# Inverting the diagonal blocks of a delta rule: one stream transpose for four blocks, TensorE in source order up to the recurrence, gates moved into the first chunks

## The chip, the cores and the metric

The kernel runs on one core of one Trainium2 chip. The time is device microseconds of one execution of the whole program; what is compared is the median of several executions. The engines are TensorE (PE in the profile: matmuls, and PEld for its weight loads), VectorE (DVE), ScalarE (ACT), GpSimd (POOL) and SyncE (SP, which issues the transfers).

## The reference

Two layers of a decoder trunk for 512 tokens of width 1024 in float32. What matters here is the mixer of each layer:

```python
n = rmsnorm(h)
p = n @ W_in              # RWKV-7 groups, MLA latents (q, kv, rope key), two groups of gates
# RWKV-7, 8 heads of 64: a state with a delta rule
state = state * w_t + (state @ a_t) b_t^T + v_t k_t^T      # a_t = -kk, b_t = kk * iclr
y_t   = state @ r_t
# MLA: 8 heads of causal softmax attention from low-rank latents
h = h + (sigmoid(g_A) * (y_A @ W_oA) + sigmoid(g_B) * (y_B @ W_oB)) @ W_out
h = h + conv_ffn(rmsnorm(h))
```

The 16 gate tiles (128 columns each of g_A and g_B) need only `n` and are read again at the end of the mixer. The attention needs the latents and no result of the delta rule.

## The kernel before, in words

Activations lie transposed, features on partitions and the 512 tokens along the free dimension. A weight unit holds eight blocks of 128 x 128; each projection of 128 columns takes one unit. To keep float32 accuracy each block and each input is split into a high and a low part, and `mm3` runs three matmuls of 512 columns per block, so a unit is 24 matmuls. `unit` and `produce` fetch a unit with SyncE into `raw` (two buffers), ScalarE casts the high part `whi` (line 201), VectorE subtracts to get `wlo` (line 202); at most two units are ready ahead. `wtile` runs a whole unit into an accumulator; `Part` does the same in pieces of n blocks (k-steps) and calls `end` on the last.

A planner orders the instructions of each engine: it simulates the engines with its own costs and, where several instructions could go, takes the one that stands first in the source. Inside `tc.manual_schedule(engines={PE.engine})` TensorE's instructions keep the order of the source; instructions from outside may still be placed among them, and the other engines remain the planner's. The kernel before uses this in three places, none of them in the stage of this change.

The delta rule is computed in 8 chunks of 64 tokens. For each chunk `c` and head, `AM` holds masked score blocks (last written at line 602), `AR` and `BT` the scaled operands, `Z` the values, `St` the states. The stage of the change stands between the four `pair` generators and the attention:

- four latent units `lat0` to `lat3` (line 658 evicts each with the norm's `rstd`), their squares, `tok_sums` on TensorE, `rsqrt_tok` (VectorE line 304, GpSimd line 305, ScalarE line 297) and `spread` (TensorE line 312), which give the two latent norms; the rope products `kp`;
- for each pair of chunks a product of the A_ak blocks with the values (line 676), copied back to `Z` by ScalarE (line 680);
- the inverse of every unit lower triangular 64 x 64 block of `AM`. The four 32 x 32 diagonal blocks (two chunk parities, two halves) are brought into `X` by stream transposes (line 698), 30 steps of forward substitution on VectorE invert them all at once (lines 702 and 704), and further transposes write them back to `AM` and into `T11` (lines 707 and 709). The lower left block is then the join: a first product with `T11` (line 718), copied to `Q` (line 721), a second product (line 725), copied into `AM` (line 729);
- the recurrence over the chunks: the state's product (line 742), its sum with `Z` (745), the inverse (751), a copy to `Z` (753), the state's update (759, 766 or 768);
- four gate units `GATES[4]`, whose eviction is line 462 and whose tanh is line 470, written to memory by SyncE.

Behind it, the attention heads (`heads`, lines 863 to 906), the chunks' outputs and their group norms. The operands of the attention (`qops`, `kvop`) are written into buffers of tag `xa`, which hold the first half of the normalized input that the gates read. `sc` has two PSUM banks, `xyt` one tile of two banks, and there are two accumulators.

Of the kernel before, what the change touches and what calls it, by code (L numbers as in the profile page):

```python
# [9 lines left out]
F32 = mybir.dt.float32  # L10
F32R = mybir.dt.float32r
I32 = mybir.dt.int32
AF = mybir.ActivationFunctionType
# [145 lines left out]
def build(ctx, tc, x, pos, wst, vecd, constd, out):  # L159
# [265 lines left out]
    def mixer(l, ops, nrm, wks):  # L425
        with ExitStack() as mx:
# [220 lines left out]
            with pool(name=f"ti{l}", bufs=2) as ti:  # L647
# [6 lines left out]
                lat = []  # L654
                for i in range(4):
                    ps = wtile(ops)
# [3 lines left out]
                sq = [ti.tile([128, 512], F32, name="lsq", bufs=3) for _ in range(3)]  # L660
                for i in range(3):
                    A.activation(sq[i], lat[i], AF.Square)
                G.tensor_tensor(sq[0], sq[0], sq[1], ALU.add)
                ws = []
                for i, (t, n) in enumerate(((sq[0], 256.0), (sq[2], 128.0))):
                    ssq = sc()
                    tok_sums(ssq, t)
                    ws.append(rsqrt_tok(ssq, n, NORM_EPS, pool=ti, tag=f"nw{i}"))


                for i in range(4):
# [10 lines left out]
                rq = tl.tile([128, 512], F32, name="rq", bufs=1)  # L682
                spread(ws[0], tabs[1], rq, sc)
                rk = ti.tile([128, 512], F32, name="rk", bufs=1)
                spread(ws[1], None, rk, sc)
                V.scalar_tensor_tensor(lat[2], lat[2], vc(l, "kv_norm"), rk, ALU.mult, ALU.mult)
                kp = tl.tile([128, 512], F32, name="kp", bufs=1)
                k2 = ti.tile([128, 512], F32, name="k2", bufs=1)
# [5 lines left out]
                X = ti.tile([128, 32, 32], F32, name="X", bufs=1)  # L694
                T11 = ti.tile([128, 32, 32], F32, name="T11", bufs=1)
                quad = [((0 if e else 64) + 32 * hf, (128 if e else 64) + 32 * hf, hf) for e in range(2) for hf in range(2)]
                for r0, c0, hf in quad:
                    V.transpose(X[r0:r0 + 32], AMu[r0:r0 + 32, :, c0:c0 + 32].rearrange("p u t -> p t u"))  # L698
                for s in range(1, 31):
                    tm = ti.tile([128, 256], F32, name="tm", tag="tm", bufs=2)  # L700
                    tm = tm[:, 0:(31 - s) * s].rearrange("p (a b) -> p a b", b=s)
                    V.tensor_tensor(tm, X[:, s + 1:32, s:s + 1].to_broadcast([128, 31 - s, s]),  # L702
                                    X[:, s:s + 1, 0:s].to_broadcast([128, 31 - s, s]), ALU.mult)
                    V.tensor_tensor(X[:, s + 1:32, 0:s], X[:, s + 1:32, 0:s], tm, ALU.add)  # L704
                V.memset(X.rearrange("p a b -> p (a b)")[:, 0:1024:33], 1.0)
# [5 lines left out]
                half = [(64, 64), (0, 128)]  # L711
                for b in range(2):
                    us = range(16 * b, 16 * b + 16)
                    Q = ti.tile([128, 512], F32, name="Q", bufs=2).rearrange("p (u s) -> p u s", s=32)
                    ps = xyt()[:, b, :]
                    for u in us:
                        for r0, c0 in half:
                            PE.matmul(ps[r0 + 32:r0 + 64, 32 * (u % 16):32 * (u % 16) + 32], AMu[r0:r0 + 32, u, c0 + 32:c0 + 64],
                                      T11[r0:r0 + 32, u, :], start=True, stop=True, tile_position=(r0, r0 + 32))
                    for r0, c0 in half:  # L720
                        (A.copy if r0 else V.tensor_copy)(Q[r0 + 32:r0 + 64], ps[r0 + 32:r0 + 64, :].rearrange("p (u s) -> p u s", s=32))
                    ps = xyt()[:, b, :]
                    for u in us:
                        for r0, c0 in half:
                            PE.matmul(ps[r0:r0 + 32, 32 * (u % 16):32 * (u % 16) + 32], Q[r0 + 32:r0 + 64, u % 16, :],
                                      AMu[r0 + 32:r0 + 64, u, c0 + 32:c0 + 64], start=True, stop=True,
                                      tile_position=(r0 + 32, r0))
                    for r0, c0 in half:
# [41 lines left out]
                for i in GATES[4][1:]:  # L770
                    gate(i, ti)
# [291 lines left out]
```

## Time and profile before

| | |
|---|---|
| Time, median of 3 runs | 1614.26 us (1613.88 to 1615.4) |
| The profiled execution's own time | 1612.19 us |
| Its span, first to last instruction | 1610.4 us |
| TensorE busy | 1571.3 us (98%) |
| VectorE busy | 939.5 us (58%) |
| ScalarE busy | 652.5 us (41%) |
| GpSimd busy | 188.3 us (12%) |
| Mean granted TensorE clock | 0.991 |

Busy time is an average over stages with different limits. The stage of the change lies at 184 to 302 us of the span in layer 0 and at 979 to 1097 us in layer 1. TensorE's matmuls are pipelined, so the duration of one is longer than the distance to the next; the clock column is the share of 2.4 GHz that TensorE was granted, and its levels are 1.2 and 2.4 GHz.

### The profile page before, as it was taken

Reading aid. Unit: us, or ns where it says so; the run is one execution under the profiler, and the core shown is the slowest. Engines: PE = TensorE matmul, PEld = TensorE weight load, DVE = VectorE, ACT = ScalarE, POOL = GpSimd, SP = SyncE. Lnnn points to the kernel's source line nnn. Section 1 sums busy time; section 2 is a strip of 40 time slices with the busy share of each in tenths; the row PEclk is TensorE's granted clock in tenths of the full one; section 3 lists DMA queues with packets and bytes.
Section 4 is the critical chain, followed back from the end, with each engine's and each line's share of the span. In section 5 each row is a group of like instructions: output and inputs, shape, how many; then the busy total and the mean of one; then the engine's idle time right before and its main releaser. Section 6 shows DMA issues by size and latency. Waiting matters only on the chain.

```text
span 1610.4 us, 22362 instructions
## 1 busy us (share of the span) xinstructions
PE 1571.3 (98%) x9036; PEld 1260.7 (78%) x9036; DVE 939.5 (58%) x1474; ACT 652.5 (41%) x988; POOL 188.3 (12%) x158
## 2 busy tenths in 40 slices
PE   8999989999999999999999999899999999999998
PEld 6888766668888888888878887666688888888887
DVE  6578796666555555533346768856665555554333
ACT  6445334573443333422245442346534443333322
POOL 1011101300211101100001110023003110110000
PEclk9999999999999999999999999899999999999999
DMA  6333312225322323233343333212343223223232
GB/s 210 111 105 125 112 60 86 67 66 156 132 92 94 102 92 102 95 106 123 111 139 110 99 98 112 73 47 80 92 145 127 94 92 99 98 92 105 92 99 85
DMA packets 57271, 166.07 MB, mean 103 GB/s; under 512 B 6352, under 2 KB 8528, under 8 KB 57168
## 3 DMA queue, kind: packets, MB, share of 16 engines
q1 hardware_dynamic: 57024, 164.48, 31.0%
q8 instruction: 71, 1.16, 0.3%
q14 instruction: 32, 0.26, 0.1%
q10 hardware_dynamic: 144, 0.16, 0.0%
HBM read 147.32 MB, written 17.30 MB: 102 GB/s over the span
## 4 chain that ended last, share of the span: by engine, by line
PE 89%; DVE 7%; POOL 2%; ACT 1%; issue 1%; DMA 0%; POOLq 0%; DVEq 0%; SPq 0%; ACTq 0%
PE acc L246 26%; PE acc L248 25%; PE acc L247 25%; PE sc L885 2%; PE po L903 2%; PE xy L751 1%; PE pt L896 1%; DVE wlo L202 1%; DVE AM L707 1%; DVE X L698 1%; POOL mu L814 1%; PE m L599 1%; DVE tm L702 1%; DVE X L704 1%; POOL Z L819 1%
## 5 line engine op out<-in xcount | busy, mean ns | idle before, releaser
L246 PE MATMUL acc<-hi,whi 128*128 128x512 f32 (+1 forms) x1910 | 752.5, 394 | 9.1 <-ACT hi L282 5.2
L248 PE MATMUL acc<-hi,wlo 128*128 128x512 f32 (+1 forms) x1910 | 746.6, 391 | 1.1 <-DVE wlo L202 1.1
L247 PE MATMUL acc<-lo,whi 128*128 128x512 f32 (+1 forms) x1910 | 745.2, 390 | 0.0
L201 ACT CAST whi<-raw 128x1024 fp32r<-128x1024 f32 (+2 forms) x249 | 253.5, 1020 | 536.9 <-PE acc L247 472.4
L246 PEld LDWEIGHTS acc<-hi,whi 128*128 128x128 f32 x1910 | 361.0, 189 | 85.3 <-ACT hi L282 5.2
L248 PEld LDWEIGHTS acc<-hi,wlo 128*128 128x128 f32 x1910 | 360.9, 189 | 78.4 <-DVE wlo L202 2.4
L247 PEld LDWEIGHTS acc<-lo,whi 128*128 128x128 f32 x1910 | 361.4, 189 | 73.6 <-issue 1.2
L202 DVE TENSOR_TENSOR wlo<-raw,whi 128x1024 fp32r<-128x1024 f32 (+2 forms) x249 | 308.3, 1240 | 175.0 <-ACT whi L201 174.4
L983 POOL TENSOR_TENSOR c<-c,rstd 128x512 f32<-128x512 f32 x44 | 57.9, 1317 | 403.6 <-ACT c L982 403.6
L976 DVE TENSOR_TENSOR u<-acc,rstd 128x512 f32<-128x512 f32 x44 | 30.4, 692 | 104.7 <-PE acc L248 104.5
L985 DVE TENSOR_TENSOR c<-c,acc 128x512 f32<-128x512 f32 x44 | 30.3, 688 | 86.4 <-POOL c L983 86.4
L982 ACT ACTIVATE c<-c 128x512 f32<-128x512 f32 x44 | 27.8, 632 | 81.7 <-DVE c L981 81.7
L341 POOL TENSOR_TENSOR nacc<-nacc,nsq 128x512 f32<-128x512 f32 x14 | 25.1, 1790 | 201.5 <-ACT nsq L340 201.5
L450 DVE TENSOR_TENSOR cur<-acc,rstd 128x512 f32<-128x512 f32 x28 | 19.1, 690 | 46.9 <-PE acc L248 39.3
L305 POOL TENSOR_TENSOR nv<-nv,cst 128x4 f32<-128x4 f32 (+1 forms) x10 | 10.1, 1011 | 309.1 <-DVE nv L304 309.1
L891 ACT ACTIVATE P<-P,mn 128x128 f32<-128x128 f32 (+3 forms) x64 | 35.6, 556 | 26.2 <-DVE mn L888 22.8
L885 PE MATMUL sc<-K,q 128*128 128x128 f32 (+3 forms) x128 | 44.5, 447 | 0.0
L462 DVE TENSOR_TENSOR gg<-acc,rstd 128x512 f32<-128x512 f32 x28 | 19.2, 685 | 35.8 <-PE acc L248 35.6
L893 ACT ACTIVATE P<-P,mn 128x128 f32<-128x128 f32 (+3 forms) x64 | 34.8, 558 | 8.8 <-DVE mn L892 8.8
L903 PE MATMUL po<-PT,Vt 128*64 128x128 f32 x320 | 37.5, 286 | 0.7 <-DVE PT L898 0.7
L979 ACT ACTIVATE c<-u,vec 128x512 f32<-128x512 f32 x44 | 35.7, 810 | 2.8 <-DVE u L975 2.8
L888 DVE CUSTOM_DVE_ANT_0 P<-sc,cst 128x128 f32<-128x128 f32 (+3 forms) x64 | 30.6, 481 | 9.1 <-PE sc L885 5.2
(240 smaller groups left out, 1396.2 us busy)
## 6 DMA issues: line engine op xcount, KB each, us to landing
raw<-in_w SPq DMA_DIRECT2D x238, 512.0 KB, 3.3
gate_d<-gg SPq DMA_DIRECT2D x32, 256.0 KB, 2.0
AM<-gate_d SPq DMA_DIRECT2D x16, 256.0 KB, 4.8
gb<-gate_d SPq DMA_DIRECT2D x16, 256.0 KB, 3.5
h<-in_x SPq DMA_DIRECT2D x8, 256.0 KB, 4.2
rgate_d<-gt SPq DMA_DIRECT2D x8, 256.0 KB, 2.6
bl_d<-rk SPq DMA_DIRECT2D x8, 256.0 KB, 2.0
bl<-bl_d SPq DMA_DIRECT2D x8, 256.0 KB, 2.7
```

The lines of the kernel that those rows point to most:

```text
L201: A.copy(hi, r)
L202: V.tensor_tensor(lo, r, hi.bitcast(F32), ALU.subtract)
L246: PE.matmul(ps, w[0], xx[0], start=first, stop=False)
L247: PE.matmul(ps, w[0], xx[1], start=False, stop=False)
L248: PE.matmul(ps, w[1], xx[0], start=False, stop=last)
L885: PE.matmul(sp[:, 0:n], qs[hh][:, 128 * b:128 * b + 128], ks[hh][:, 0:n], start=True, stop=True)
L888: V.tensor_tensor_reduce(out=P[:, 0:n], in0=sp[:, 0:n], in1=cst[:, C_CAUS + 512 - n:C_CAUS + 512], scale=-ATT_SCALE, scalar=1e30, op0=ALU. ...
L891: A.activation(P[:, 0:n], P[:, 0:n], AF.Exp, bias=mn[:, 0:1], scale=-1.0, accum_out=mn[:, 1:2])
L893: A.activation(P[:, 0:n], P[:, 0:n], AF.Copy, scale=mn[:, 2:3])
L903: PE.matmul(po[64 * hh:64 * hh + 64, 128 * b:128 * b + 128], Vt[:, kb, 64 * hd:64 * hd + 64], PTs[hh][:, 128 * kb:128 * kb + 128], start=k ...
L979: A.activation(cc, u[:, 2:514], AF.Identity, bias=vc(l, "conv_b", i), scale=vc(l, "conv_w", 2 * FT + i))
L983: G.tensor_tensor(cc, cc, rstd, ALU.mult)
```

## The change

- **One transpose for four blocks.** The four diagonal blocks are first copied side by side into a tile `DX` of 128 partitions, two copies on VectorE and two on ScalarE. One stream transpose of all 128 partitions brings them into `X`, one gives `T11` and one gives `T22`, the inverse in its original orientation. `back` copies `T22` into `AM` on ScalarE, two copies for each chunk parity. The second joining product reads `T22` instead of `AM`. The substitution now stands first in the stage's source.
- **TensorE in source order.** The whole stage, up to and with the recurrence, stands in a `manual_schedule` region for TensorE: three latent units, an A_ak product, sums, the fourth latent in two halves, sums, spread, A_ak, spread, half a gate, A_ak, half a gate, A_ak, a gate, the join with parts of a gate between, the recurrence. The sum of the first two squares is taken by TensorE's accumulation instead of GpSimd.
- **Joining copies.** Both copies of `Q` for each half are on VectorE; of the copies into `AM` one half is ScalarE's and the other VectorE's. Both products for the two halves run one behind the other in `sc` banks.
- **Gates in the first chunks.** The last half of one gate and a whole one are issued two k-steps at a time by `filler`, once behind each of the recurrence's product groups, until they are used up in the third chunk.

```diff
-            with pool(name=f"ti{l}", bufs=2) as ti:
+            with pool(name=f"ti{l}", bufs=2) as ti, tc.manual_schedule(engines={PE.engine}):
+                DX = ti.tile([128, 32, 32], F32, name="DX", tag="dx", bufs=1)
...
+                for r0, c0, hf in quad:
+                    (A.copy if hf else V.tensor_copy)(DX[r0:r0 + 32], AMu[r0:r0 + 32, :, c0:c0 + 32])
+                V.transpose(X, DX.rearrange("p u t -> p t u"))
+                for s in range(1, 31):
...
+                V.memset(X.rearrange("p a b -> p (a b)")[:, 0:1024:33], 1.0)
+                V.transpose(T11.rearrange("p u s -> p s u"), X.rearrange("p t s -> p s t"))
+                T22 = ti.tile([128, 32, 32], F32, name="T22", tag="dx", bufs=1)
+                V.transpose(T22.rearrange("p u t -> p t u"), X)
+                def back(e):
+                    for r0, c0, hf in quad:
+                        if (r0 < 64) == bool(e):
+                            A.copy(AMu[r0:r0 + 32, :, c0:c0 + 32], T22[r0:r0 + 32])
+                back(0)
...
-                G.tensor_tensor(sq[0], sq[0], sq[1], ALU.add)
...
+                def lsum(i, t, n):
+                    ssq = sc()
+                    tok_sums(ssq, t)
+                    return rsqrt_tok(ssq, n, NORM_EPS, pool=ti, tag="lsq", bufs=3)
...
+                parts4 = [Part(ops, lat_end) for _ in range(4)] + [gpart(i) for i in GATES[4]]
+                for i in range(3):
+                    parts4[i].go()
+                a_ak_v(0)
+                w0 = lsum(0, sq[0:2], 256.0)
+                parts4[3].go(4)
+                w1 = lsum(1, sq[2], 128.0)
+                parts4[3].go()
...
+                spread(w0, tabs[1], rq, sc)
+                a_ak_v(1)
...
+                spread(w1, None, rk, sc)
...
+                parts4[4].go(4)
+                a_ak_v(2)
+                parts4[4].go()
+                a_ak_v(3)
+                parts4[5].go()
...
-                for r0, c0, hf in quad:
-                    V.transpose(X[r0:r0 + 32], AMu[r0:r0 + 32, :, c0:c0 + 32].rearrange("p u t -> p t u"))
...
-                for r0, c0, hf in quad:
-                    V.transpose(AMu[r0:r0 + 32, :, c0:c0 + 32].rearrange("p u t -> p t u"), X[r0:r0 + 32])
-                    if hf == 0:
-                        V.transpose(T11[r0:r0 + 32].rearrange("p u s -> p s u"), X[r0:r0 + 32].rearrange("p t s -> p s t"))
-                gate(GATES[4][0], ti)
...
                     for r0, c0 in half:
-                        (A.copy if r0 else V.tensor_copy)(Q[r0 + 32:r0 + 64], ps[r0 + 32:r0 + 64, :].rearrange("p (u s) -> p u s", s=32))
...
+                        V.tensor_copy(Q[r0 + 32:r0 + 64], ps[r0 + 32:r0 + 64, :].rearrange("p (u s) -> p u s", s=32))
+                    Qs.append(Q)
+                parts4[6].go(2)
...
+                            PE.matmul(ps[r0:r0 + 32, 32 * (u % 16):32 * (u % 16) + 32], Qs[b][r0 + 32:r0 + 64, u % 16, :],
+                                      T22[r0 + 32:r0 + 64, u, :], start=True, stop=True, tile_position=(r0 + 32, r0))
...
+                for r0, c0 in half:
+                    for b in range(2):
+                        (V.tensor_copy if b else A.copy)(AMu[r0:r0 + 32, 16 * b:16 * b + 16, c0 + 32:c0 + 64],
+                                                         pss[b][r0:r0 + 32, :].rearrange("p (u s) -> p u s", s=32))
+                back(1)
+                parts4[6].go(2)
...
+                rest = iter([(parts4[6], 2)] * 2 + [(parts4[7], 2)] * 4)
+                def filler():
+                    for part, n in (next(rest, (None, 0)),):
+                        if part:
+                            part.go(n)
...
                                           St[c][k0:k0 + 64, p, :], start=True, stop=True, tile_position=(k0, ur))
+                        filler()
...
                                   xs[ur:ur + 64, hd, :], start=True, stop=True, tile_position=(ur, ur))
+                    filler()
...
                                           Z[:, i, e, 64 * hd:64 * hd + 64], start=True, stop=True, tile_position=(0, 64 * hh))
+                        filler()
...
-                for i in GATES[4][1:]:
-                    gate(i, ti)
```

## Rows read from the trace of the kernel before

**Rows 1.** The page, busy time, share of the span, instructions.
```profile
PE 1571.3 (98%) x9036; PEld 1260.7 (78%) x9036; DVE 939.5 (58%) x1474; ACT 652.5 (41%) x988; POOL 188.3 (12%) x158
```

**Rows 2.** Layer 0 by stretch: length; PE, PEld, DVE, ACT, POOL busy; clock; DMA.
```profile
193.91:230.63 36.72, 32.59 (x253) 26.28 (x252) 32.69 (x79) 12.94 (x19) 4.09 (x3) 0.95 0.24 79
230.63:242.23 11.60, 7.33 (x90) 5.51 (x88) 11.49 (x6) 2.68 (x3) 0.00 (x0) 1.00 0.01 2
242.23:256.20 13.97, 13.13 (x219) 10.08 (x219) 8.75 (x12) 5.83 (x9) 0.00 (x0) 0.76 0.34 115
256.20:302.00 45.80, 44.52 (x485) 31.92 (x484) 27.73 (x69) 21.27 (x50) 8.63 (x13) 1.00 0.16 53
302.00:362.00 60.00, 57.72 (x536) 38.87 (x535) 40.88 (x119) 41.27 (x96) 13.15 (x11) 1.00 0.25 79
```

**Rows 3.** The same in layer 1, for the stretch before the recurrence.
```profile
1037.18:1051.37 14.19, 13.36 (x220) 10.27 (x221) 8.82 (x12) 5.90 (x9) 0.00 (x0) 0.76 0.33 113
```

**Rows 4.** TensorE's waits from 183.8 to 256.2: us in total, times, longest.
```profile
PE sc L312 <- ACT nw L297: 3.8, 2, 3.2
PE xy L718 <- DVE T L709: 3.6, 2, 1.9
PE acc L246 <- DVE gg L462: 1.5, 1, 1.5
```

**Rows 5.** Busy time by stretch from 242 to 250, columns as in rows 2.
```profile
242.00:250.00 8.00, 6.93 (x76) 5.24 (x76) 7.06 (x10) 4.05 (x7) 0.00 (x0) 0.57 0.40 139
```

**Rows 6.** Timeline of TensorE: start, us, engine, line, operation, tiles.
```profile
183.81 0.48 PE L246 MATMUL acc<-hi,whi 128*128 128x512 f32 x1
...
192.75 0.39 PE L246 MATMUL acc<-hi,whi 128*128 128x512 f32 x1
...
194.11 0.39 PE L246 MATMUL acc<-hi,whi 128*128 128x512 f32 x1
```

**Rows 7.** The chain that ended last, from 184 to 258: start, us.
```profile
222.76 1.08 PE xy L676 x32
...
250.14 1.13 PE xy L718 x64
```

**Rows 8.** TensorE's groups from 183.8 to 256.2: busy us, mean ns.
```profile
L325 PE MATMUL sc<-cst,lsq 128*128 128x1 f32 x16 | 1.8, 245 | 0.0
```

**Rows 9.** Stream transposes of X and T, layer 0: min, median, max ns.
```profile
L698 DVE STREAM_TRANSPOSE X<-AM x4: 2011/2018/2026, 185.8 to 191.9; 32x1024 f32<-32x1024 f32 x4
...
L709 DVE STREAM_TRANSPOSE T<-X x2: 1868/1911/1954, 232.5 to 238.3; 32x1024 f32<-32x1024 f32 x2
```

**Rows 10.** VectorE's groups from 193.9 to 230.6: busy, mean ns, idle before.
```profile
L704 DVE TENSOR_TENSOR X<-X,tm 128x30 f32<-128x30 f32 (+14 forms) x30 | 11.0, 368 | 0.8
L702 DVE TENSOR_TENSOR tm<-X 128x30 f32<-128x30 f32 (+14 forms) x30 | 9.9, 330 | 0.9
L202 DVE TENSOR_TENSOR wlo<-raw,whi 128x1024 fp32r<-128x1024 f32 x5 | 6.1, 1217 | 0.0
...
L686 DVE SCALAR_TENSOR_TENSOR lat<-lat,vec,rk 128x512 f32<-128x512 f32 x1 | 0.8, 751 | 1.1 <-ACT rk L316 1.1
...
L462 DVE TENSOR_TENSOR gg<-acc,rstd 128x512 f32<-128x512 f32 x1 | 0.7, 691 | 1.1 <-PE acc L248 1.1
```

**Rows 11.** VectorE's groups from 230.6 to 256.2, columns as above.
```profile
L721 DVE COPY Q<-xy 32x512 f32<-32x512 f32 x2 | 1.4, 684 | 1.6 <-ACT Q L721 1.6
```

**Rows 12.** ScalarE's groups from 180 to 260, by form.
```profile
L201 ACT CAST whi<-raw 128x1024 fp32r<-128x1024 f32 x9 | 9.4, 1045 | 20.3 <-PE acc L247 20.2
```

**Rows 13.** Timeline of TensorE at the second step of the recurrence.
```profile
259.85 0.68 PE L742 MATMUL xy<-St,AR 64*64 64x64 f32 x16 [0.99 <-DVE St L768]
```

**Rows 14.** Timeline of VectorE while the rope tables are made.
```profile
133.81 0.49 DVE L372 TENSOR_SCALAR ang<-ang,cst 128x512 f32<-128x512 f32 x1
134.21 0.68 DVE L450 TENSOR_TENSOR cur<-acc,rstd 128x512 f32<-128x512 f32 x1
134.81 0.42 DVE L373 TENSOR_SCALAR ang<-ang 128x512 f32<-128x512 f32 x1
```

More of the change, by code (lines that the diff above doesn't have):

```diff
@@ L653, in mixer, with lat_end @@
                     tabs.append(t)
-                lat = []
-                for i in range(4):
-                    ps = wtile(ops)
+                lat, sq = [], []
+                def lat_end(ps):
+                    i = len(lat)
                     o = (tl if i < 3 else ti).tile([128, 512], F32, name=f"lat{i}", bufs=1)
@@ L659, in mixer, with a_ak_v @@
                     lat.append(o)
-                sq = [ti.tile([128, 512], F32, name="lsq", bufs=3) for _ in range(3)]
-                for i in range(3):
-                    A.activation(sq[i], lat[i], AF.Square)
-                G.tensor_tensor(sq[0], sq[0], sq[1], ALU.add)
[L664 to L671, printed above, removed]
+                    if i < 3:
+                        sq.append(ti.tile([128, 512], F32, name="lsq", tag="lsq", bufs=3))
+                        A.activation(sq[i], o, AF.Square)
+                def a_ak_v(i):
                     ps = xyt()
@@ L680, in mixer, with gpart, end @@
                         A.copy(Z[ur:ur + 64, i, e, :], ps[ur:ur + 64, e, :])
[L682 to L686, printed above, removed]
+                def lsum(i, t, n):
+                    ssq = sc()
+                    tok_sums(ssq, t)
+                    return rsqrt_tok(ssq, n, NORM_EPS, pool=ti, tag="lsq", bufs=3)
+                def gpart(i):
+                    def end(ps):
+                        gg = ti.tile([128, 512], F32, name="gg", tag="gg", bufs=2)
+                        V.tensor_tensor(gg, ps, rstd, ALU.mult)
+                        gate_out(i, gg)
+                    return Part(ops, end)
+                parts4 = [Part(ops, lat_end) for _ in range(4)] + [gpart(i) for i in GATES[4]]
[6 more added lines that the diff above has]
+                parts4[3].go()
                 kp = tl.tile([128, 512], F32, name="kp", bufs=1)
-                k2 = ti.tile([128, 512], F32, name="k2", bufs=1)
+                k2 = ti.tile([128, 512], F32, name="k2", tag="lsq", bufs=3)
                 V.tensor_tensor(kp[64:128, :], lat[3][0:64, :], tabs[0][0:64, :], ALU.mult)
@@ L699, in mixer @@
[L699 to L705, printed above, removed]
@@ L711, in mixer @@
+                spread(w1, None, rk, sc)
+                V.scalar_tensor_tensor(lat[2], lat[2], vc(l, "kv_norm"), rk, ALU.mult, ALU.mult)
+                parts4[4].go(4)
[3 more added lines that the diff above has]
+                parts4[5].go()
                 half = [(64, 64), (0, 128)]
+                Qs, pss = [], []
                 for b in range(2):
[L713 to L714 removed]
@@ L715, in mixer @@
-                    ps = xyt()[:, b, :]
-                    for u in us:
+                    ps = sc()
+                    for u in range(16 * b, 16 * b + 16):
                         for r0, c0 in half:
-                            PE.matmul(ps[r0 + 32:r0 + 64, 32 * (u % 16):32 * (u % 16) + 32], AMu[r0:r0 + 32, u, c0 + 32:c0 + 64],
-                                      T11[r0:r0 + 32, u, :], start=True, stop=True, tile_position=(r0, r0 + 32))
+                            PE.matmul(ps[r0 + 32:r0 + 64, 32 * (u % 16):32 * (u % 16) + 32],
+                                      AMu[r0:r0 + 32, u, c0 + 32:c0 + 64], T11[r0:r0 + 32, u, :],
+                                      start=True, stop=True, tile_position=(r0, r0 + 32))
@@ L720, in mixer @@
+                    Q = ti.tile([128, 16, 32], F32, name="Q", tag="Q", bufs=2)
                     for r0, c0 in half:
[L721 to L727 removed]
@@ L728, in mixer @@
-                    for r0, c0 in half:
-                        (A.copy if r0 else V.tensor_copy)(AMu[r0:r0 + 32, 16 * b:16 * b + 16, c0 + 32:c0 + 64],
-                                                          ps[r0:r0 + 32, :].rearrange("p (u s) -> p u s", s=32))
-                St = [None]
+                        V.tensor_copy(Q[r0 + 32:r0 + 64], ps[r0 + 32:r0 + 64, :].rearrange("p (u s) -> p u s", s=32))
+                    Qs.append(Q)
+                parts4[6].go(2)
+                for b in range(2):
+                    ps = sc()
+                    for u in range(16 * b, 16 * b + 16):
+                        for r0, c0 in half:
+                            PE.matmul(ps[r0:r0 + 32, 32 * (u % 16):32 * (u % 16) + 32], Qs[b][r0 + 32:r0 + 64, u % 16, :],
+                                      T22[r0 + 32:r0 + 64, u, :], start=True, stop=True, tile_position=(r0 + 32, r0))
+                    pss.append(ps)
```

14 lines of the change are left out of this document (11 added, 3 removed).

## The prediction

> **What bounds the kernel now.** I read the page first: TensorE is busy in 98% of the span [rows 1], so only time in which it idles, or works at the lower of its two clocks, can be won. Then the table of stretches, laid over the stage that the diff touches. It shows both losses in the 70 us from the last masked score tile (185.77) to the first step of the recurrence (256.20), and little in the 46 us of the recurrence, where TensorE is busy for 44.5 [rows 2]. VectorE is busy for 32.69 of 36.72 us, then for 11.49 of 11.60: in this stage VectorE sets the pace. Layer 1 repeats it; its stretch ahead of the recurrence has the same clock and is 0.2 us longer [rows 3].
>
> The waits say what ends TensorE's idle time [rows 4]: 3.8 us for the norm columns to be spread, 3.6 for the transposed block T, 1.5 for a gate's eviction. The clock is the other loss: a granted 0.95 over 36.72 us and 0.76 over 13.97 [rows 2] are 1.8 and 3.4 us; the stretch from 242 to 250 stands at 0.57, so mostly at 1.2 instead of 2.4 GHz [rows 5], right behind the idle gaps at the transposes.
>
> What the stage needs at full speed: the projections' matmuls start 0.227 us apart (six in 1.36 us) [rows 6], so a unit of 24 takes 5.44 and eight units 43.5. Four products of A_ak and V at 1.08 and four joining products at 1.13 [rows 7] are 8.8, token sums 1.8 [rows 8], two spreads about 1.3, three value matmuls 0.7. That is 56.1 us; from the first unit (183.8, [rows 6]) to 256.2 there are 72.4. So 16.3 us per layer are lost, 32.6 in all: the most that this change can give here.
>
> **Transposes.** Before, the diagonal blocks take four stream transposes of 32 partitions to enter X, four to return and two for T, at 2.0 and 1.9 us [rows 9], all on VectorE. Now four copies gather the blocks (two on VectorE, two on ScalarE), three transposes of 128 partitions do the rest, and ScalarE copies the return. No row shows a transpose of 128 partitions. Bounds: 2.0 us if time follows the elements per partition, 8.0 if it follows the partitions. I take 2.0: with 512 elements per partition, a gate's eviction of 128 partitions takes 0.69 us [rows 10] and a joining copy of 32 takes 0.68 [rows 11].
>
> The Trainium skill (Vector Engine (DVE) Microarchitecture Reference, section 3.8) gives each bank of 32 lanes a transposing array of its own, at one element per cycle and lane; that agrees with taking 2.0 rather than 8.0. But by this rate 1024 elements would need about 1.1 us at the 0.96 GHz of VectorE: DVE Perf Modes (Specifications), an estimate from the two pages. The 2.0 of the rows disagrees and decides; by the pages X and T would come 1.8 us sooner per layer and the total would be about 3.6 us lower.
>
> The gathering copies have no row either. ScalarE moves 1024 elements in 1.05 us [rows 12], so its two take 2.1; VectorE's two lie between 1.4 (twice a 512-element copy, [rows 11]) and 2.5 (twice the 1.22 of a 1024-element weight split, [rows 10]). ScalarE has the slack. X then stands at 185.77 + 2.1 to 2.5 + 2.0 = 189.9 to 190.3, where it was 193.91.
>
> **The substitution on VectorE.** Its 60 instructions (11.0 + 9.9 us) and the evictions, splits and rope products between them stay: 36.72 us from X to its end [rows 2, 10], of which 1.1 and 1.1 were waits. So 34.5 to 36.7 more: 224.4 to 227.0. One transpose gives T for both halves: 226.4 to 229.0, where the second T was ready at 240.3. I take 228.
>
> **TensorE up to the join.** Source order puts four latent units and two gates (32.6 us) ahead of it, four A_ak products (4.3), the sums, two spreads (1.3). The sums now read two squared tiles instead of one that GpSimd added up: 24 instead of 16 instructions, 1.8 becomes 2.7 [rows 8]. With a tenth of a us at each of some twelve switches of tile shape that is 183.8 + 42 = 225.8. VectorE's 228 still ends last, by about 2 us; no transfer does, since each weight unit is loaded two units ahead.
>
> **The join.** First products 2.3 us; meanwhile VectorE makes T22 (2.0, to 230.0), then four copies of Q at 0.68 (to 232.7). Two k-steps of gate 14 cover 1.4 of it on TensorE. Second products end at about 234; the last copies (0.7 on VectorE, ScalarE beside it) lie under two more k-steps of 1.4. Recurrence at 228 + 7.4 = 235.4. Two possible delays: a weight split and a gate eviction ahead of Q on VectorE (1.22 + 0.69 = 1.9), and the lower clock behind the remaining gap: between 0 and the 3.4 us it costs now. I take 1.5 for the two together, nearer to nothing because one gap of 2 us replaces three of 1.5 to 1.9 [rows 4]. That is 236.9.
>
> ScalarE's four return copies cost 4.2 us; two are due before the first step and lie under the join, two before the second, under the first step's 3.7 us (256.20 to 259.85 before, [rows 2, 13]) and its fillers. Late, they would add up to 1 us per layer.
>
> **What is deferred.** At 256.2 all four gates and three value matmuls were done. Now one and a half gates remain, 12 k-steps or 8.2 us, plus 0.7. They are the fillers of the first chunks: 1.36 us each into gaps of about 1 us (TensorE now sits idle for 0.99 ahead of the second step [rows 13]), so they cost their own work and no more. The earlier start is worth 256.2 - 8.9 - 236.9 = 10.4 us per layer. What follows is the same TensorE work, 97 and 96% busy [rows 2]; with more attention left over to cover GpSimd's normalizing I count no change.
>
> **The rivals.**
> *TensorE held in its order.* In source order a sum or a spread whose operand is late holds the gates behind it. For it: the spread waited up to 3.2 us [rows 4] while a gate's matmuls stood behind it. Against it: VectorE was late there by the 8 us of transposes into X, now 4 shorter. If two such waits of 2.5 us stay and land past VectorE's pace, 5 of the 10.4 are lost: about 1604.
> The Trainium skill (TensorE: Matmul & The Clock Gate, Part 3, The mechanism) states that matmuls start and end strictly in program order; the trace agrees, with that wait of 3.2 us.
>
> *Covers missing later.* The gates used to be done before the recurrence, which the attention heads fill. The query and value operands reuse buffers of the normalized input, so they wait for the last gate, now in the second chunk. If chunks two to four lack fillers, some nine gaps of 0.5 us and a later first head cost 3 to 6 us per layer: about 1603. Against it: some 6 us of value and projection matmuls come first and need no softmax.
>
> *The other side: VectorE starved by the substitution.* The substitution now stands ahead of the latent evictions in the source. If the planner runs its 60 dependent instructions and two transposes without a break, evictions and splits wait from 190 to 190 + 22 + 4 = 216. TensorE has weights for two units, until 195, and idles for 21 us; its other 31 us before the join end at 247, the recurrence starts at 254, 7 later than the 247.3 (256.2 - 8.9) that compares: 1628. It decides once splits lag by more than two units. Against it: the rope tables' chain is of this kind, and an eviction of a later projection slipped in between two of its dependent instructions [rows 14].
>
> *Transposes by partitions* (8.0 us each): X 6 later, T at 240, T22 at 248, the recurrence near 253.5: about 1626. The equal times across partition counts speak against it.
>
> **How the numbers follow.** The profiled execution took 1612.19 us around its span; the median of the runs shown, 1614.26, is 2.07 above it. Two layers at 10.4 give 20.8: 1591.4 for the profile's own time, 1593.5 on the median's scale, as are the rivals' times. This case's own range: T at 226.4 and no delay, recurrence at 233.8, 13.5 per layer, 1587; T at 229.0 with 1.9 and 3.4, at 241.7, 5.6 per layer, 1603.
> Chances: forecast 0.62; held in order 0.15; covers missing 0.10; starved 0.06; by partitions 0.03; mixtures near no change 0.04. To take in the two middle rivals and a little on either side, the range is 1584 to 1608. 0.2% is 3.2 us, about what a measurement can tell. Faster: 0.62 and nearly all of 0.25, 0.84. Slower: 0.06 + 0.03 + 0.01 = 0.10. The same: 0.06.
>
> **What would show it.** Right: three transposes per layer of about 2.0 us on 128 partitions; T about 42 us behind the last score tile instead of 54.5; the recurrence about 51 us behind it instead of 70; no TensorE wait for T above 3 us; a granted clock above 0.9 in the join; gate matmuls in the first three chunks. Wrong: a transpose of 4 us or more; waits of TensorE on evictions or norm columns that add up to over 5 us; idle time in chunks two to four; a substitution without foreign instructions in it.

## The result, and the profile after

The changed kernel takes 1593.38 us (median of 4 runs, 1591.89 to 1593.9), the kernel before beside it 1614.83. The ratio is 0.9866 with a 95% interval of 0.9849 to 0.9883, so it is faster by 1.3%; the forecast was 1593.5. Its profiled execution took 1593.16 us around a span of 1591.4. That the median came out within 0.2 us of the forecast is partly luck: two terms of the sum were off by about 3 us per layer each, in opposite directions.

Stretches of layer 0 (start:end and length in us, then the busy time of TensorE, its weight loads, VectorE, ScalarE and GpSimd, the granted clock, and the share and rate of the DMA engines). They begin at the end of X's transpose, at the start of T's, and at the first step of the recurrence, and answer to [rows 2]:

```profile
191.84:225.41 33.57, 33.57 (x271) 27.84 (x270) 31.07 (x79) 13.49 (x20) 2.27 (x2) 1.00 0.25 79
225.41:235.64 10.23, 9.61 (x277) 7.67 (x276) 9.87 (x10) 6.90 (x8) 0.00 (x0) 1.00 0.19 64
235.64:284.40 48.76, 47.19 (x481) 33.74 (x480) 27.61 (x60) 20.70 (x43) 8.04 (x12) 1.00 0.19 64
```

TensorE is busy in all of the first stretch and idles for 0.62 us in the second. The granted clock is 1.00 throughout, 2.4 GHz, where the join had 0.76 before. VectorE is still nearly full up to the join (31.07 of 33.57, 9.87 of 10.23), so the two engines now arrive almost together.

VectorE's work from the last masked score tile on, in order of time (start, duration, instruction, idle time before it):

```profile
186.26 1.28 DVE L602 TENSOR_TENSOR AM<-m,cst 128x512 f32<-128x512 f32 x2
187.58 1.38 DVE L654 COPY DX<-AM 32x1024 f32<-32x1024 f32 x2
189.71 2.10 DVE L655 STREAM_TRANSPOSE X<-DX 128x1024 f32<-128x1024 f32 x1 [0.76 <-ACT DX L654]
...
192.41 0.22 DVE L659 TENSOR_TENSOR tm<-X 128x58 f32<-128x58 f32 x1
192.55 0.68 DVE L685 TENSOR_TENSOR lat<-acc,rstd 128x512 f32<-128x512 f32 x1
193.15 0.21 DVE L661 TENSOR_TENSOR X<-X,tm 128x58 f32<-128x58 f32 x1
...
225.41 2.18 DVE L663 STREAM_TRANSPOSE T<-X 128x1024 f32<-128x1024 f32 x1
227.46 1.95 DVE L665 STREAM_TRANSPOSE T<-X 128x1024 f32<-128x1024 f32 x1
229.24 0.69 DVE L710 TENSOR_TENSOR gg<-acc,rstd 128x512 f32<-128x512 f32 x1
229.96 2.82 DVE L751 COPY Q<-sc 32x512 f32<-32x512 f32 x4
```

A transpose of 128 partitions takes 1.95 to 2.18 us, about as long as one of 32 [rows 9]. The score tile ends at 187.54, X at 191.8, and the first transpose behind the substitution (L663) at 227.6. It now gives T for both halves, 40.0 us behind the tile; before, the second half's T came at 54.5. An eviction of a latent unit (L685) stands between the two instructions of one substitution step, so that VectorE was not closed to TensorE's evictions.

TensorE at the join and at the first chunks:

```profile
227.65 2.21 PE L746 MATMUL sc<-T,AM 32*32 32x32 f32 x128 [0.34 <-DVE T L663]
...
232.93 1.20 PE L758 MATMUL sc<-T,Q 32*32 32x32 f32 x64 [0.22 <-DVE Q L751]
...
235.64 1.14 PE L795 MATMUL xy<-Z,AM 64*64 64x64 f32 x16
236.71 0.50 PE L246 MATMUL acc<-hi,whi 128*128 128x512 f32 x1
237.05 0.39 PE L247 MATMUL acc<-lo,whi 128*128 128x512 f32 x1
```

The recurrence starts at 235.64, 48.1 us behind the score tile (70.5 before). Layer 1 repeats it: 49.0 us (70.7 before). In layer 0 the start moved by 22.4 us, but the first split of the feed-forward network came only 10.3 us sooner, counted from the score tile (454.5 less 187.54 against 463.0 less 185.73). Of the 12.1 us between, 8.9 are the gates and value matmuls that were moved behind the start, as forecast; 3.2 are a new loss. The whole layer, from the last score tile of layer 0 to that of layer 1, took 784.5 us instead of 794.9, so 10.4 us less; the rest of the span behind layer 1's tile fell by 10.5. What TensorE waited for from the join to the end of the mixer (total us, times, longest):

```profile
PE xy L869 <- POOL Z L863: 1.2, 1, 1.2
PE pt L940 <- DVE mn L936: 0.7, 1, 0.7
PE xy L795 <- DVE xs L789: 0.7, 1, 0.7
PE xy L833 <- ACT Z L844: 0.7, 2, 0.3
PE xy L869 <- ACT Z L844: 0.6, 1, 0.6
PE xy L785 <- DVE St L812: 0.6, 1, 0.6
PE sc L929 <- DVE q L921: 0.5, 1, 0.5
PE sc L746 <- DVE T L663: 0.3, 1, 0.3
```

Of these only the last stands ahead of the recurrence (with 0.2 us for Q, in the rows above); the waits of [rows 4] for norm columns and gates have gone, and that for T has nearly gone. Behind the recurrence's start TensorE had short waits before the change too, for the state (1.0 us) and for the outputs' values from GpSimd and ScalarE (1.7 and 0.6). What is new are 0.7 us inside the recurrence (L795), 0.7 at the outputs (L833) and 1.2 at the heads (L929, L940).

### The profile page after: what moved, and what is told of

It is laid out like the page before. It is cut to its first block, busy times and chain, and to the rows that moved or that the text cites. A ratio compares the mean times of both kernels' runs of the same rounds, so it can differ in the third digit from the quotient of the medians.

```text
span 1591.4 us, 22441 instructions
## 1 busy us (share of the span) xinstructions
PE 1562.6 (98%) x9052; PEld 1254.2 (79%) x9052; DVE 915.4 (58%) x1468; ACT 661.5 (42%) x996; POOL 184.7 (12%) x156
## 4 chain that ended last, share of the span: by engine, by line
PE 91%; DVE 4%; issue 2%; ACT 1%; POOL 1%; DMA 0%; SPq 0%; POOLq 0%; DVEq 0%; ACTq 0%
PE acc L246 26%; PE acc L247 26%; PE acc L248 26%; PE sc L929 2%; PE po L947 2%; PE pt L940 1%; PE m L599 1%; PE xy L795 1%; DVE wlo L202 1%; PE m L607 1%; PE m L583 0%; PE xy L804 0%; PE m L524 0%; DVE X L661 0%; POOL mu L858 0%
## 5 line engine op out<-in xcount | busy, mean ns | idle before, releaser
L246 PEld LDWEIGHTS acc<-hi,whi 128*128 128x128 f32 x1910 | 359.6, 188 | 82.5 <-ACT hi L282 5.2
L929 PE MATMUL sc<-K,q 128*128 128x128 f32 (+3 forms) x128 | 44.6, 446 | 1.1 <-DVE q L921 1.1
L932 DVE CUSTOM_DVE_ANT_0 P<-sc,cst 128x128 f32<-128x128 f32 (+3 forms) x64 | 30.7, 483 | 12.9 <-PE pt L940 10.4
L947 PEld LDWEIGHTS po<-PT,Vt 128*64 128x64 f32 x320 | 22.3, 136 | 18.2 <-issue 7.3
```

Source lines behind the costliest of these rows:

```text
L246: PE.matmul(ps, w[0], xx[0], start=first, stop=False)
L929: PE.matmul(sp[:, 0:n], qs[hh][:, 128 * b:128 * b + 128], ks[hh][:, 0:n], start=True, stop=True)
L932: V.tensor_tensor_reduce(out=P[:, 0:n], in0=sp[:, 0:n], in1=cst[:, C_CAUS + 512 - n:C_CAUS + 512], scale=-ATT_SCALE, scalar=1e30, op0=ALU. ...
L947: PE.matmul(po[64 * hh:64 * hh + 64, 128 * b:128 * b + 128], Vt[:, kb, 64 * hd:64 * hd + 64], PTs[hh][:, 128 * kb:128 * kb + 128], start=k ...
```

## The experiments

Each kernel is the changed one with one edit, unless said otherwise. The changed kernel run again beside the first group took 1592.23 us (0.987, 0.9855 to 0.9884), and is the yardstick. Ratios are all to the kernel before on the same chip. The three groups ran on three chips, where the kernel before took 1613.54, 1612.48 and 1612.05 us, so times of different groups compare to within 1 to 1.5 us.

> The changed kernel once more, on the chip of the variants that follow, as their yardstick. Every theory: 1592 to 1595 us, 21 below the kernel before.

**The transposes undone.** Ten transposes of 32 partitions in the new order of the stage:

```diff
-                    (A.copy if hf else V.tensor_copy)(DX[r0:r0 + 32], AMu[r0:r0 + 32, :, c0:c0 + 32])
-                V.transpose(X, DX.rearrange("p u t -> p t u"))
+                    V.transpose(X[r0:r0 + 32], AMu[r0:r0 + 32, :, c0:c0 + 32].rearrange("p u t -> p t u"))
...
+                for r0, c0, hf in quad:
+                    V.transpose(AMu[r0:r0 + 32, :, c0:c0 + 32].rearrange("p u t -> p t u"), X[r0:r0 + 32])
+                    if hf == 0:
+                        V.transpose(T11[r0:r0 + 32].rearrange("p u s -> p s u"), X[r0:r0 + 32].rearrange("p t s -> p s t"))
...
```

> The changed kernel with the ten transposes of 32 partitions put back and the copies around DX and T22 taken out; source order, joining copies and gates in the chunks stay. Theory 1, VectorE's way to T sets the start of the join: X about 4 us later, the second T about 7.5 us later, nothing in TensorE's fixed order fills the wait, so 9 to 12 us per layer and a lower granted clock in the join: 1611 to 1620. Rival, the order of TensorE gives most of the gain: 1596 to 1604. A TensorE wait for T of 8 us or more would speak for theory 1.

Measured: 1622.8 us, ratio 1.0054 (1.0039 to 1.0069), slower than the kernel before and than theory 1's range, whose sign, a wait of 8 us or more, is there. TensorE's order of time around the join of this kernel:

```profile
232.65 0.31 PE L738 MATMUL sc<-T,AM 32*32 32x32 f32 x2 [4.03 <-DVE T L664]
...
238.23 3.62 PE L738 MATMUL sc<-T,AM 32*32 32x32 f32 x126 [5.26 <-DVE T L664]
```

TensorE waits 9.3 us for T, and the products behind the wait take 3.62 us where the changed kernel needs 2.21. So the rest of the change without the transposes (order, joining copies and deferred gates together) is a loss of about 9 us against the kernel before: while T is late, TensorE has nothing to do.

**The transposes alone,** put into the kernel before (two small tiles share other buffers, for space):

```diff
-                    V.transpose(X[r0:r0 + 32], AMu[r0:r0 + 32, :, c0:c0 + 32].rearrange("p u t -> p t u"))
+                    (A.copy if hf else V.tensor_copy)(DX[r0:r0 + 32], AMu[r0:r0 + 32, :, c0:c0 + 32])
+                V.transpose(X, DX.rearrange("p u t -> p t u"))
...
```

> The kernel before with the gathering copies, the three transposes of 128 partitions and ScalarE's return copies alone; the planner still orders TensorE, the gates stay ahead of the recurrence. Theory 1, VectorE's way to T is most of it: 7 to 11 us per layer, 1593 to 1601, with a wait of 1 to 3 us for the norm columns left over. Rival, without the fixed order the planner leaves TensorE waiting elsewhere: 1604 to 1611.

Measured: 1602.17 us, 0.993 (0.9914 to 0.9947), between the ranges of the two theories: a gain of 11.4 us, about half. TensorE's longest waits in layer 0, and its stretches behind the first of them and at the first steps of the recurrence (length, busy time, granted clock, DMA):

```profile
PE sc L312 <- ACT nw L297: 2.1, 2, 1.8
PE xy L721 <- DVE T L708: 1.4, 1, 1.4
```
```profile
212.00:224.00 12.00, 11.17 (x131) 1.00 0.14 45
256.00:260.00 4.00, 3.43 (x33) 0.52 0.24 91
```

The other half needs the rest of the change: minus 11.4 for one part and plus 9.3 for the other become minus 21.3 together. They are not to be added.

**TensorE's written order taken away.**

```diff
-            with pool(name=f"ti{l}", bufs=2) as ti, tc.manual_schedule(engines={PE.engine}):
+            with pool(name=f"ti{l}", bufs=2) as ti:
```

> The changed kernel without the region that fixes TensorE's order; all else stays. Theory 1, with the transposes short the waits for the norm columns nearly vanish by themselves: 1593 to 1598. Rival, the fixed order is what removes those waits: 1600 to 1608, with waits of 3 us and more for the norm columns or the evictions.

Measured: 1590.93 us, 0.9862 (0.9847 to 0.9877), overlapping with the yardstick and below what either theory gave. The planner takes what stands first in the source, and TensorE's order up to the recurrence comes out the same, matmul by matmul. The rewritten source does the work; the region itself adds nothing that can be measured.

**The substitution at its old place in the source,** behind the latent units and the rope products instead of ahead of them (the block is moved, unchanged):

```diff
-                DX = ti.tile([128, 32, 32], F32, name="DX", tag="dx", bufs=1)
...
-                back(0)
...
                 V.scalar_tensor_tensor(lat[2], lat[2], vc(l, "kv_norm"), rk, ALU.mult, ALU.mult)
                 parts4[4].go(4)
                 a_ak_v(2)
                 parts4[4].go()
                 a_ak_v(3)
                 parts4[5].go()
+                DX = ti.tile([128, 32, 32], F32, name="DX", tag="dx", bufs=1)
...
+                back(0)
```

> The changed kernel with the gathering copies, the substitution and its transposes moved back to their old place in the source, behind the rope products and the norms; all else stays. If the planner lets any ready instruction slip between dependent ones, the place decides little: 1591 to 1596. If the place in front keeps VectorE on the way to T, T comes 2 to 4 us later per layer and TensorE waits for it: 1597 to 1601.

Measured: 1595.9 us, 0.9895 (0.9879 to 0.9911). TensorE's wait for T is 1.1 us instead of 0.3 in layer 0 (1.0 instead of 0.4 in layer 1). The place is worth a few us at most; against the yardstick the intervals overlap a little.

**How tightly T limits.** The first transpose for T is made twice:

```diff
+XTRA = 1
...
                 V.transpose(T11.rearrange("p u s -> p s u"), X.rearrange("p t s -> p s t"))
+                for _ in range(XTRA):
+                    V.transpose(T11.rearrange("p u s -> p s u"), X.rearrange("p t s -> p s t"))
```

> The changed kernel with the transpose that makes T11 done twice, one more VectorE instruction of 2.1 us on the way to the join. Theory 1, VectorE's T is what the join waits for, by 0.3 us already: the join starts 2.1 us later in each layer, 4 us in all and a little clock: 1596 to 1599. Rival, TensorE itself is the limit by now and VectorE has slack: 1592 to 1594.

Measured: 1604.93 us, 0.9948 (0.9933 to 0.9963), 12 us slower for 2 x 2.1 us of work, and more than theory 1 expected. TensorE at the join:

```profile
229.66 3.58 PE L749 MATMUL sc<-T,AM 32*32 32x32 f32 x128 [3.91 <-DVE T L666]
```

The wait of 0.34 us became 3.91, and the products behind it take 3.58 instead of 2.21: the delay is paid once as idle time and again in clock (a granted 0.50 from 230 to 234). VectorE still sets T, and TensorE arrives just ahead of it.

**Work taken off VectorE.** If VectorE sets T, less of its other work should help. The three rope products go to GpSimd, and GpSimd adds the two squared tiles, so that TensorE has eight sums fewer:

```diff
-                w0 = lsum(0, sq[0:2], 256.0)
+                G.tensor_tensor(sq[0], sq[0], sq[1], ALU.add)
+                w0 = lsum(0, sq[0], 256.0)
...
-                V.tensor_tensor(kp[64:128, :], lat[3][0:64, :], tabs[0][0:64, :], ALU.mult)
+                G.tensor_tensor(kp[64:128, :], lat[3][0:64, :], tabs[0][0:64, :], ALU.mult)
...
```

> The changed kernel with the three rope products for the key moved from VectorE to GpSimd, and the sum of the first two squares made by GpSimd again instead of TensorE. Both engines' ways to the join get shorter: VectorE's by three instructions of 0.69, TensorE's by the eight extra token sums, 0.9 us. The join should start 0.9 to 1.4 us earlier per layer: 1589.5 to 1591.5. If neither is the limit: 1592 to 1593.5. If GpSimd's products come too late for the heads or hold its other work: 1593 to 1596.

Measured: 1600.1 us, 0.9923 (0.9908 to 0.9938), slower by 8 us and above every range expected. T came no sooner: 40.6 us behind the score tile. Three views show why: VectorE's order of time, GpSimd's, and the durations of the substitution's additions (L661, ns: minimum, median, maximum).

```profile
198.49 1.45 DVE L661 TENSOR_TENSOR X<-X,tm 128x198 f32<-128x198 f32 x1
...
212.31 2.31 DVE L202 TENSOR_TENSOR wlo<-raw,whi 128x1024 fp32r<-128x1024 f32 x1
```
```profile
197.91 1.81 POOL L718 TENSOR_TENSOR lsq<-lsq 128x512 f32<-128x512 f32 x1 [23.29 <-ACT lsq L689]
...
212.22 1.32 POOL L726 TENSOR_TENSOR k<-lat,tab 64x512 f32<-64x512 f32 x1
213.62 2.15 POOL L727 TENSOR_TENSOR kp<-kp,k 64x512 f32<-64x512 f32 x1
```
```profile
L661 DVE TENSOR_TENSOR X<-X,tm x60: 191/350/1454, 190.3 to 1012.7; 128x30 f32<-128x30 f32 x4, 128x58 f32<-128x58 f32 x4, 128x84 f32<-128x84 f32 x4, 128x108 f32<-128x108 f32 x4
```

The same view of the changed kernel:

```profile
L661 DVE TENSOR_TENSOR X<-X,tm x60: 191/350/410, 192.2 to 1009.7; 128x30 f32<-128x30 f32 x4, 128x58 f32<-128x58 f32 x4, 128x84 f32<-128x84 f32 x4, 128x108 f32<-128x108 f32 x4
```

An addition that takes 0.36 us in the changed kernel takes 1.45 while GpSimd adds its tiles and ends 0.2 us behind it; a weight split of 1.22 takes 2.31 beside two GpSimd products. The groups of layer 0's substitution stretch sum it up: steps 11.5 + 11.0 us against 9.9 + 9.9, five splits 7.1 against 6.1, together 3.7 us more, which eats the 2.1 us of products removed. The Trainium skill (SBUF — State Buffer, Who interferes with whom) says that a VectorE instruction with two inputs in SBUF contends with a GpSimd instruction that reads SBUF; the trace agrees, with the 1.45 beside 0.36. TensorE meanwhile arrived earlier than T, waited 1.82 us, and ran behind it for 8 us at a granted clock of 0.58 and 0.56:

```profile
226.38 3.45 PE L747 MATMUL sc<-T,AM 32*32 32x32 f32 x128 [1.82 <-DVE T L663]
```
```profile
226.00:230.00 4.00, 3.62 (x129) 0.58 0.18 70
230.00:234.00 4.00, 4.00 (x71) 0.56 0.24 77
```

**The joining copies shared as before,** one of each pair on ScalarE:

```diff
-                        V.tensor_copy(Q[r0 + 32:r0 + 64], ps[r0 + 32:r0 + 64, :].rearrange("p (u s) -> p u s", s=32))
+                        (A.copy if r0 else V.tensor_copy)(Q[r0 + 32:r0 + 64], ps[r0 + 32:r0 + 64, :].rearrange("p (u s) -> p u s", s=32))
...
-                        (V.tensor_copy if b else A.copy)(AMu[r0:r0 + 32, 16 * b:16 * b + 16, c0 + 32:c0 + 64],
+                        (A.copy if r0 else V.tensor_copy)(AMu[r0:r0 + 32, 16 * b:16 * b + 16, c0 + 32:c0 + 64],
```

> The changed kernel with the joining copies shared as before: of each pair of Q copies one on VectorE and one on ScalarE, and the same for the copies of the joined quarter. Theory A (the copies are a small term either way: two VectorE copies of 0.68 in a row against one of 0.68 beside one of about 0.8 on ScalarE): within 1.5 us of the changed kernel, 1591 to 1594.5, with a TensorE wait for Q below 1 us. Theory B (a copy on ScalarE stands behind a weight split of 1.05 us or a return copy of 1.05 us, so Q comes late): a TensorE wait for Q of 1 us or more per layer, the lower clock behind it, 1595 to 1602.

Measured: 1600.4 us, 0.993 (0.9917 to 0.9944), theory B. ScalarE in order of time, then TensorE, then the clock in layer 0 and, last, in layer 1:

```profile
227.49 2.10 ACT L670 COPY AM<-T 32x1024 f32<-32x1024 f32 x2 [1.26 <-DVE T L665]
229.62 0.63 ACT L470 ACTIVATE gg<-gg 128x512 f32<-128x512 f32 x1
230.27 1.06 ACT L751 COPY Q<-sc 32x512 f32<-32x512 f32 x2
```
```profile
231.62 2.73 PE L758 MATMUL sc<-T,Q 32*32 32x32 f32 x128 [2.14 <-DVE Q L751]
```
```profile
234.00:238.00 4.00, 4.00 (x28) 0.50 0.01 4
238.00:242.00 4.00, 4.00 (x19) 0.50 0.00 0
1026.00:1030.00 4.00, 4.00 (x24) 0.72 0.01 4
```

ScalarE's copies of Q stand behind two return copies and a gate's tanh. TensorE waits 2.14 us for Q in both layers, instead of 0.22 in layer 0 of the changed kernel. In layer 0 at least 8 us then pass at 0.50, 1.2 GHz; in layer 1 the clock is 0.72 over 4 us and 1.00 behind them. This small part of the change is worth 8 us, but unevenly: in the profiled execution it is 7.3 us from layer 0's last score tile to layer 1's, and 1.9 us from there to the end.

**All gates ahead of the recurrence,** as before, and nothing deferred:

```diff
-                rest = iter([(parts4[6], 2)] * 2 + [(parts4[7], 2)] * 4)
+                parts4[6].go()
+                parts4[7].go()
+                rest = iter(())
```

> The changed kernel with all of the four gates issued ahead of the recurrence, none in its chunks; all else stays. Theory 1, the gates in the first chunks cost their own work and no more, and what is given back behind the recurrence is not theirs: 1590 to 1594, as the changed kernel. Theory 2, they are the cover that the first chunks have, because value matmuls and attention cannot start in time: the recurrence starts 8 us later, chunks one to four show waits of 0.3 to 1 us and a lower clock, 2 to 4 us per layer: 1596 to 1601.

Measured: 1584.27 us, 0.9826 (0.9809 to 0.9844), 8 us faster than the changed kernel (7 by the ratios) and better than what either theory gave. So the fourth part of the change costs about 4 us per layer. Three more kernels ask how.

**The same 12 k-steps in twelve stops, in two stops, and ahead without the written order** (a stop is a place in the recurrence where `filler` is called; the changed kernel uses six):

```diff
-                rest = iter([(parts4[6], 2)] * 2 + [(parts4[7], 2)] * 4)
+                rest = iter([(parts4[6], 1)] * 4 + [(parts4[7], 1)] * 8)
```

> The 12 deferred gate k-steps go one at a time into the first twelve stops of the recurrence, instead of two at a time into the first six; all else as in the changed kernel. The runs so far: with all gates ahead of the recurrence 1584.3, with six stops 1592 to 1593, so 8 us for six stops in two layers. Theory A (each stop filled by a gate is a stop that is no longer there to cover the waits of the value, projection and head matmuls, which cannot begin before the last gate has ended; cost goes by the number of stops, 1.3 us each over both layers): twelve stops give about 1600, the first value matmul of a layer moves from the third chunk to the fifth, and more idle time stands behind the recurrence. Theory B (what costs is that two k-steps, 1.36 us, are longer than a gap of about 1 us): one k-step of 0.7 us fits, about 1585 to 1588. Theory C (only the switches of matmul shape cost, 0.2 us for each stop): about 1594.6.

```diff
-                rest = iter([(parts4[6], 2)] * 2 + [(parts4[7], 2)] * 4)
+                rest = iter([(parts4[6], 4), (parts4[7], 8)])
```

> The 12 deferred gate k-steps go into the first two stops of the recurrence, four into the first and eight into the second. Theory A (a stop taken by a gate is lost as cover for what follows the last gate, 1.3 us each over both layers): about 1587, most of the way to the 1584.3 with all gates ahead. Theory B (a filler longer than its gap costs what it is longer by): the 8.2 us stand in two gaps of 1 us, some 6 us per layer uncovered against 2 us with six stops: about 1600. Theory C (0.2 us for each stop's shape switches): about 1590.6.

```diff
-            with pool(name=f"ti{l}", bufs=2) as ti, tc.manual_schedule(engines={PE.engine}):
+            with pool(name=f"ti{l}", bufs=2) as ti:
...
-                rest = iter([(parts4[6], 2)] * 2 + [(parts4[7], 2)] * 4)
+                parts4[6].go()
+                parts4[7].go()
+                rest = iter(())
```

> All gates ahead of the recurrence and TensorE free of the written order: the two edits that were faster alone. If they add up, 1584.3 less 1.3 is about 1583. If the order is needed where all gates stand ahead (another instruction slips ahead of the join), 1585 to 1590 with new TensorE waits at the join.

Measured: 1584.35 us (0.9828, 0.9815 to 0.9842) with twelve stops, 1587.71 (0.985, 0.9836 to 0.9863) with two, 1586.42 (0.984, 0.9827 to 0.9854) ahead without the order; the last interval overlaps with that of 1584.27, so the order's worth stays unproven here too.

None of the three theories holds for all. A loses at twelve stops, B at two (1587.7, not 1600), C at both. TensorE's busy time from the first step of the recurrence to the end of its last matmul or just behind it, and from there to the heads' last product; the changed kernel, then gates ahead, twelve stops, two stops:

```profile
235.64:284.40 48.76, 47.19 (x481) 1.00 0.19 64
284.40:354.00 69.60, 65.48 (x581) 1.00 0.28 85
```
```profile
242.33:288.70 46.37, 45.55 (x488) 1.00 0.16 53
288.70:346.60 57.90, 55.60 (x528) 1.00 0.24 74
```
```profile
234.40:275.20 40.80, 39.47 (x433) 1.00 0.23 76
275.20:346.40 71.20, 70.16 (x619) 1.00 0.22 68
```
```profile
234.50:286.00 51.50, 50.42 (x509) 1.00 0.18 60
286.00:347.80 61.80, 59.66 (x543) 1.00 0.27 82
```

Idle time in the two stretches together is 1.57 + 4.12 = 5.7 us in the changed kernel, and 3.1, 2.4 and 3.2 in the other three (before: 1.28 + 2.28 = 3.6, [rows 2]). That is 2.6, 3.3 and 2.5 us less, where layer 0 as a whole, from score tile to score tile, is 3.6, 3.9 and 2.5 us shorter than in the changed kernel. So idle time is most of what they gain. (By its ratio alone the kernel with two stops can't be told from the yardstick; its profiled execution is 2.5 and 2.8 us shorter in the two layers.) Most of the changed kernel's idle time stands behind the recurrence. A reading of it is that heads and outputs have too little TensorE work between their waits there, and that the variants avoid this in two ways. With gates ahead or in two stops the first score of a head comes earlier than in the changed kernel (70.1 and 73.8 us behind the score tile, against 76.9), so the heads run beside the recurrence. With twelve stops it comes later (82.5), but the recurrence's last product comes at 87.6 us instead of 95.6, since one k-step lets the next step start after 0.7 us and not 1.4; more of the heads is left to cover the outputs. Two k-steps at six stops have neither. This reading fits all four kernels but was formed after them; no run tests it.

## Why the prediction came out right

**Transposes: right.** 2.1 and 2.18 us against 2.0, X 4.3 us behind the score tile as forecast (4.1 to 4.5); VectorE's copies took 1.38 of the 1.4 to 2.5, ScalarE's two 2.1. The rival that time goes by partitions falls. The time by the Trainium skill's rate (Vector Engine (DVE) Microarchitecture Reference, section 3.8), an estimated 1.1 us, falls as well: the rows of 128 partitions show 1.95 to 2.18.

**The substitution: shorter than the bound.** 33.57 us against 34.5 to 36.7, and T at 40.0 instead of 42. I kept both sets of 30 steps at [rows 10] and missed that GpSimd's addition of the squared tiles had stretched one step of that set: the longest addition was 1431 ns before and is 410 now, and the 30 additions fell from 11.0 to 9.9 us. The kernel before, VectorE and GpSimd:

```profile
201.04 1.43 DVE L704 TENSOR_TENSOR X<-X,tm 128x168 f32<-128x168 f32 x1
```
```profile
200.49 1.78 POOL L663 TENSOR_TENSOR lsq<-lsq 128x512 f32<-128x512 f32 x1 [25.84 <-ACT lsq L662]
```

Removing a GpSimd instruction, which I had priced only by the eight sums it adds on TensorE, paid 1.1 us on VectorE.

**TensorE up to the join: right in kind.** Forecast was T last by about 2 us; it is last by 0.34, since T came 2 us sooner than forecast while TensorE was ready 39.8 us behind the tile, as forecast (40.0). The doubled transpose shows that T does come last.

**The join: right, with the delays too high.** T to the recurrence took 8.0 us, forecast 7.4 + 1.5. A split and an eviction did stand among the copies, but with waits of 0.34 and 0.22 us the clock stayed at 1.00, so that the share for the lower clock fell away. What that share could have been, the doubled transpose, the GpSimd kernel and the old copies show: with waits of 3.9, 1.8 and 2.1 us at the join the lower clock came, for stretches of different length.

**What is deferred: right as work, wrong as cover.** The prediction took 8.9 us and let the fillers "cost their own work and no more", and of what follows it said "I count no change". These are the steps that failed. Behind the recurrence's start the time grew by 12.1 us, 3.2 more than that: 2.1 of idle time (5.7 against 3.6), and 1.1 whose cause stays open. A switch of matmul shape costs about 0.1 us (237.05 less 236.71 is 0.34 us, where neighbours of one shape start 0.227 apart [rows 6]), but the fillers bring no more of them: from the recurrence's start to the feed-forward network's first split the trace has 106 changes of shape in layer 0, and 107 before. The rival "Covers missing later" named a loss of this kind, with 3 to 6 us per layer, but gave it 0.10 as an alternative to the forecast; it came beside it. It also looked for the idle time in chunks two to four: the recurrence idles for 1.6 us against 1.3 before, and 4.1 against 2.3 stand behind it. In layer 0 the start was 13.5 us earlier net of the 8.9, where 10.4 were forecast; less 3.2 that is 10.3. Two layers give 20.6, and the span fell by 19.0, since layer 0's last score tile came 1.8 us later in this execution.

**The other rivals.** TensorE held in its order: no wait for norm columns or latent evictions is left in the stage, and taking the order away moved the time by 1.3 us, inside the intervals. VectorE starved: evictions slipped in between the steps.

## What to carry to other kernels

When a slow producer is shortened, rewrite the order of its consumer with it: here the transposes alone were worth minus 11 us, the rest alone plus 9, both together minus 21, and a wait of some 2 us left at the join was paid again in clock, by amounts that differ between the layers of one kernel. Work that is moved into the gaps of a dependent chain is not free by that: here 12 k-steps in six gaps cost 8 us more than ahead of the chain. It may take the place of other cover: look at how long a filler holds the chain's next step, and at what is left to cover the waits behind the chain's end, before counting the move as free. The version to keep is the change without its deferral, or with one k-step in each gap, at 1584.3 us (ratio 0.983).

## What the runs showed of the hardware beyond expectation

The granted clock behind a wait of TensorE does not follow from the length of the wait alone. A wait of 1.8 us for T was followed by 0.58 and 0.56 over 8 us (the GpSimd kernel), and the same wait of 2.14 us for Q by 0.50 over at least 8 us in layer 0 and by 0.72 over 4 us in layer 1 (the old copies). With the transposes alone, the wait of 1.8 us for norm columns left the clock at 1.00 in layer 0 and was followed by 0.72 over 6 us in layer 1, and three waits of 0.3 to 0.8 us within 4 us at the first steps of the recurrence were followed by 0.52; in the changed kernel waits of 0.6 to 0.7 us there left it at 1.00. What decides between them no run here shows.

A two-input instruction of VectorE that started while an elementwise instruction of GpSimd was running ended about 0.2 us behind it in two cases: 1.45 us instead of 0.36 (the GpSimd kernel), 1.43 where the steps around it take 0.33 to 0.35 (the kernel before). Not every overlap costs: a weight split that had begun ahead of that addition (199.90 in the kernel before) kept its 1.22 us, and substitution steps beside GpSimd's instructions on 128 x 4 values (206.5 to 209.8 in the changed kernel) kept their 0.41.

A copy of 1024 float32 elements on 32 partitions took VectorE 0.68 us, no longer than one of 512 out of PSUM (0.69), and ScalarE 1.05.
